# Twelve modulation pieces of a two-block transformer kernel redistributed over VectorE, TensorE and two later places

## The chip, the core and the metric

The kernel runs on one core of one Trainium2 chip. The metric is the device time of one execution in microseconds (us), as the median of several runs. Engines are named as the profile names them: PE is TensorE, PEld its weight loads, DVE is VectorE, ACT is ScalarE, POOL is GpSimd, SP is SyncE, whose queue issues nearly all weight loads. One launch computes the whole model; the weights (380 MB are moved in all, most of it the experts) come from HBM as they are needed.

## What is computed

Two blocks on T = 256 tokens of width D = 1024, everything in float32. Ahead of each block stands a modulation: six vectors ("pieces") of 1024 numbers, each one the product of a 1024-vector with a 1024 x 1024 slice of a weight.

```python
mod = jax.nn.silu(c) @ w_ada[l] + b_ada[l]                   # block one; c_2, w_ada_2, b_ada_2 for block two
sh1, sc1, g1, sh2, sc2, g2 = jnp.split(mod[:, None, :], 6, axis=-1)
h = layer_norm(x) * (1.0 + sc1) + sh1
mix = hybrid_mixer(h, w_in, ...)                             # state-space scan (SSD), short conv, gates, w_o
x = layer_norm(ALPHA * x + g1 * mix) * ln1_g + ln1_b
h = layer_norm(x) * (1.0 + sc2) + sh2
ffn = moe_ffn(h, ...)                                        # router, 8 of 64 experts, a shared expert
x = layer_norm(ALPHA * x + g2 * ffn) * ln2_g + ln2_b
...
h = modulate(rms_norm(x), shift_mix, scale_mix)              # block two
mixed = concat([rms_norm(attn_a) * g_a, rms_norm(attn_b) * g_b]) @ w_out
x = x + gate_mix * mixed
h = modulate(rms_norm(x), shift_ffn, scale_ffn)
gate, val = split(causal_depthwise_conv(h @ w_up, conv_w, conv_b), 2)
x = rms_norm(x + gate_ffn * ((silu(gate) * val) @ w_down)) * final_g
```

A piece is written (b, n) below: b = 0 or 1 for the block, n = 0 to 5 in the order of the split. So (0,2) is g1, (1,0) is shift_mix, (1,2) is gate_mix, (1,3) is shift_ffn, (1,5) is gate_ffn.

## The kernel before

The program is one straight line of stages, each bound to a stretch of the span: modulation (0,0) and (0,1) and the input norm (0 to 37 us); x, the 16 projections that feed the SSD scan (37 to 146); s, 12 projections with the scan's steps woven in (146 to 242); o, the 4 projections `pyb` of the short convolution's output, still with scan steps (242 to 286); z (286 to 342); g, the gates (342 to 396); u, the SSD output projection (396 to 443); `pmix`, the product with w_o, then the first norm and the router (443 to 492); the mixture of experts (492 to 976); the turn to block two, with its norm and the transposes `hb_tp` (976 to 1006); projections and two attentions (1006 to 1140); the up projection with 22 products (1140 to 1269); the down projection and the final norm (1269 to 1339).

A projection is `lin_fm` (L554 to L556): for each of 16 tiles three matmuls, hi x hi, lo x hi and hi x lo. Weights come in float32 and are split on the way: ACT copies the upper part (`whi`, L194) and DVE subtracts it (`wlo`, L198), both per 128 x 1024 half of a 1 MB tile.

Loads go through the class `Stream` (L28). Requests are put in a list in program order; `pump` issues them on SP strictly in that order, each as soon as a buffer of its ring is free: 5 buffers `wraw`, and around the experts 6 `mraw` and 3 `whl`. A request that finds no free buffer holds up all that follow. SP's order is the written one. On the other engines the order of instructions is fixed when the program is built, by a scheduler that may move independent instructions, and each engine executes its queue in order: an instruction that waits holds up all that stand behind it on its engine.

A modulation piece has two forms. Form one is on PE (`ada_piece`, L394, matmuls L403): for each of the four 1 MB tiles of the piece 8 matmuls with the silu(c) column, spread to 32 columns in the constant tile `cst` (L184), as the stationary operand. It is used for (0,0) and (0,1). Form two is on DVE (`ada_tick`, L406): for each of the piece's 8 rows of 128 one SCALAR_TENSOR_TENSOR accumulates weight x silu(c) into `adac` (L430); the first row is done on ACT (L428); at the end PE sums over the partitions with a ones matrix (L435), DVE adds the bias (L390) and ACT's queue writes the 4 KB result to `mod_scr` in HBM (L459). Whoever needs the piece reads it back from there through POOL's queue. In form two a tile is loaded where a string of 0 and 1 says so, one digit for each projection of the stages x, s, o, z, g and u, and consumed at the same place:

```python
XS, SS, OS, ZS, GS, US = [[int(c) for c in a] for a in
                          "0110110110110110,010101010101,1111,11111111,11111111,10101010".split(",")]
```

So 10 pieces, 40 tiles of 1 MB, go through DVE there: 10 tiles in x, 6 in s, 4 in o, 8 in z, 8 in g and 4 in u.

At the turn SP's list holds the last experts' tiles, the two rows of the second norm (`ln2`), the relative-position bias (two gathers from `rel_scr`, L1259 and L1260, into an `mraw` buffer) and the tiles of w_in_2 (L213). PE turns the bias into `bt` (L1659); ACT splits the first w_in_2 tile (L194), takes the squares of the norm (L1683) and scales (L1687); POOL raises to the power -0.5 (L1685); PE transposes `hb_tp` (L1695); ACT and DVE make `hb_f`, `hbh` and `hbl` from it (L493, L494, L486); then the first product `pqb` of block two starts.

Of the kernel before, what the change touches and what calls it, by code (L numbers as in the profile page):

```python
# [25 lines left out]
D = 1024  # L26
# [8 lines left out]
class Stream:  # L35
# [86 lines left out]
def build(ctx, tc, I, out, dbg=None, stop=None):  # L122
# [61 lines left out]
    cst = glob.tile([128, 8, 32], F32, name="cst")  # L184
    V.tensor_copy(cst, csil[:, :8, None].to_broadcast([128, 8, 32]))
# [59 lines left out]
    def req_ada_tile(b, piece, k0):  # L245
        w = I["w_ada_2" if b else "w_ada"][0]

        def f(t):
            n = 2 if (b, piece, k0) == (0, 1, 6) else 1
# [7 lines left out]
        ada_q[b, piece, k0] = ws.add(f, None)  # L257

    def req_ada(b, piece):
        for k0 in range(0, 8, 2):  # L260
# [8 lines left out]
                              "0110110110110110,010101010101,1111,11111111,11111111,10101010".split(",")]  # L269
# [122 lines left out]

    def ada_piece(b, pc):
# [3 lines left out]
        for k0 in range(0, 8, 2):  # L397
            i = ada_q[b, pc, k0]
            w = ws.take_raw(i)
            wv = w.rearrange("p (k n) -> p k n", k=2)  # L400
            for k in range(2):
                for j in range(4):
                    PE.matmul(p[32 * j:32 * j + 32, :256], cst[:, 8 * b + k0 + k, :], wv[:, k, 256 * j:256 * j + 256],  # L403
                              start=(k0 + k == 0), stop=(k0 + k == 7), tile_position=(0, 32 * j))
            ws.done(i)
# [357 lines left out]
    for i in range(4):  # L763
# [365 lines left out]
    rstd(a0, 1e-5)  # L1129
    b0 = first_shift(0, a0)  # L1130
# [4 lines left out]
    G.dma_start(g2, bsrc(scr[5]))  # L1135
    first_scale(1, a1)
# [14 lines left out]
    pr0 = logits(0)  # L1151

# [10 lines left out]
    neg_exp(0, pr0)  # L1163
    scores(0)
# [348 lines left out]
    def prepare_loads():  # L1513

        for k, pc in enumerate((0, 1, 3, 4)):
# [211 lines left out]
    def proj_fm(nm, scale):  # L1727
# [165 lines left out]
    G.dma_start(gfx[:, 0, :], bsrc(scr[11]))  # L1893
# [19 lines left out]
    for i in range(11):  # L1913
# [17 lines left out]
        defer(evac_v)  # L1931
    flush()
# [53 lines left out]
```

## Time and profile before

| what | value |
|---|---|
| median of 3 runs | 1338.19 us (1337.98 to 1346.47) |
| the profiled execution's own time | 1340.41 us |
| its span, first to last instruction | 1338.5 us |
| outside the span | 1.91 us |
| PE busy | 1268.3 us, 95% of the span |
| DVE busy | 813.3 us, 61% |
| ACT, POOL busy | 562.1 us, 178.9 us |
| mean granted clock of PE | 0.979 of full speed |
| moved by DMA | 380.18 MB, 284 GB/s over the span |

The table is an average over stages with different limits. [...]

### The profile page before, as it was taken

Reading aid. Unit: us, or ns where it says so; the run is one execution under the profiler, and the core shown is the slowest. Engines: PE = TensorE matmul, PEld = TensorE weight load, DVE = VectorE, ACT = ScalarE, POOL = GpSimd, SP = SyncE. Lnnn points to the kernel's source line nnn. Section 1 sums busy time; section 2 is a strip of 40 time slices with the busy share of each in tenths; the row PEclk is TensorE's granted clock in tenths of the full one; section 3 lists DMA queues with packets and bytes.
Section 4 is the critical chain, followed back from the end, with each engine's and each line's share of the span. In section 5 each row is a group of like instructions: output and inputs, shape, how many; then the busy total and the mean of one; then the engine's idle time right before and its main releaser. Section 6 shows DMA issues by size and latency. Waiting matters only on the chain.

```text
span 1338.5 us, 22545 instructions
## 1 busy us (share of the span) xinstructions
PE 1268.3 (95%) x8998; PEld 1029.2 (77%) x8998; DVE 813.3 (61%) x1306; ACT 562.1 (42%) x849; POOL 178.9 (13%) x169
## 2 busy tenths in 40 slices
PE   4999999999999989999999999999979999999997
PEld 1898988788899777657576767476549876999986
DVE  2899998977898862222322222222264677788995
ACT  0666644445654342313131313132245655666643
POOL 1002233421100000211112111112120000000000
PEclk9899999999999979999999999999998999899999
DMA  9977766759889288999999999999995334455450
GB/s 337 306 248 252 255 218 225 244 192 311 259 283 345 89 331 314 399 417 418 418 418 416 402 415 419 377 420 403 417 344 177 126 126 138 146 189 185 164 187 32
DMA packets 148975, 380.18 MB, mean 284 GB/s; under 512 B 7839, under 2 KB 97285, under 8 KB 129028
## 3 DMA queue, kind: packets, MB, share of 16 engines
q1 hardware_dynamic: 145856, 373.20, 75.3%
q0 software_dynamic: 2240, 5.34, 1.2%
q8 instruction: 71, 1.16, 0.4%
q10 hardware_dynamic: 772, 0.19, 0.1%
q14 instruction: 36, 0.29, 0.1%
HBM read 377.59 MB, written 1.10 MB: 283 GB/s over the span
## 4 chain that ended last, share of the span: by engine, by line
PE 62%; DVE 5%; DMA 4%; issue 1%; ACT 1%; POOL 0%; SPq 0%; DVEq 0%; POOLq 0%; ACTq 0%
PE gu L1442 16%; PE dn L1473 8%; PE xgp L1400 5%; PE sc L1495 4%; PE pgt L554 2%; PE pgt L555 2%; PE pgt L556 2%; PE pvl L554 2%; PE pvl L556 2%; PE pvl L555 2%; PE pf L906 1%; PE pf L908 1%; PE pf L904 1%; DVE wlo L198 1%; DMA wraw<-in_w_down_dram 1%
## 5 line engine op out<-in xcount | busy, mean ns | idle before, releaser
L194 ACT ACTIVATE whi<-wraw 128x1024 fp32r<-128x1024 f32 x216 | 228.1, 1058 | 244.2 <-PE pf L908 30.8
L198 DVE TENSOR_TENSOR wlo<-wraw,whi 128x1024 fp32r<-128x1024 f32 x216 | 271.3, 1258 | 68.0 <-ACT whi L194 66.6
L1442 PE MATMUL gu<-mraw,xg 128*32 128x256 f32 (+2 forms) x976 | 135.1, 381 | 0.0
L1483 POOL TENSOR_TENSOR y<-yf,y 128x512 fp32r<-128x512 f32 x60 | 76.8, 1280 | 420.9 <-ACT y L1482 420.8
L1452 DVE SCALAR_TENSOR_TENSOR act<-act,gc,gu 128x256 f32<-128x256 f32 x31 | 14.9, 480 | 192.9 <-ACT act L1451 192.9
L1482 ACT ACTIVATE y<-yf 128x512 fp32r<-128x512 f32 x62 | 39.0, 630 | 160.3 <-DVE yf L1481 160.3
L1442 PEld LDWEIGHTS gu<-mraw,xg 128*32 128x32 f32 (+2 forms) x976 | 86.7, 135 | 22.7 <-issue 5.3
L1442 PE MATMUL gu<-wraw,xg 128*32 128x256 f32 (+2 forms) x704 | 98.7, 381 | 0.0
L1481 DVE TENSOR_TENSOR yf<-dn,g 128x512 f32<-128x512 f32 x62 | 42.9, 692 | 66.1 <-PE dn L1473 66.1
L556 PE MATMUL pl<-hh,wlo 128*128 128x256 f32 x256 | 74.4, 292 | 4.2 <-DVE wlo L198 4.1
L1442 PEld LDWEIGHTS gu<-wraw,xg 128*32 128x32 f32 (+2 forms) x704 | 58.2, 129 | 24.1 <-issue 3.9
L555 PE MATMUL pl<-hl,whi 128*128 128x256 f32 x256 | 73.8, 288 | 0.0
L554 PE MATMUL pl<-hh,whi 128*128 128x256 f32 x256 | 73.7, 288 | 0.0
L430 DVE SCALAR_TENSOR_TENSOR adac<-wraw,csil,adac 128x1024 f32<-128x1024 f32 x49 | 66.6, 1359 | 5.1 <-DMA wraw<-in_w_ada_dram 4.6
L1495 PE MATMUL sc<-y,S 128*128 128x512 f32 x248 | 63.3, 404 | 1.4 <-ACT y L1482 0.8
L1495 PEld LDWEIGHTS sc<-y,S 128*128 128x128 f32 x248 | 45.5, 188 | 17.6 <-issue 4.4
L1451 ACT ACTIVATE act<-gu 128x256 f32<-128x256 f32 x31 | 11.9, 383 | 107.3 <-PE gu L1442 107.3
L1402 ACT ACTIVATE xg<-xgp,mvp 128x512 f32<-128x512 f32 (+1 forms) x64 | 48.8, 764 | 18.7 <-PE xgp L1400 18.5
L1400 PE MATMUL xgp<-D,x2h 128*128 128x512 f32 (+1 forms) x128 | 55.0, 429 | 1.4 <-DVE D L1119 1.4
L1473 PE MATMUL dn<-mraw,aT 128*32 128x512 f32 (+2 forms) x200 | 55.2, 596 | 0.0
L556 PEld LDWEIGHTS pl<-hh,wlo 128*128 128x128 f32 x256 | 49.6, 194 | 6.2 <-DVE wlo L198 5.8
L1400 PE MATMUL xgp<-D,x2l 128*128 128x512 f32 (+1 forms) x128 | 53.0, 414 | 0.4 <-DVE x2l L1069 0.4
(575 smaller groups left out, 3531.7 us busy)
## 6 DMA issues: line engine op xcount, KB each, us to landing
wraw<-in_w_in_dram SPq DMA_DIRECT2D x56, 1024.0 KB, 6.4
wraw<-in_w_ada_dram SPq DMA_DIRECT2D x47, 1024.0 KB, 7.2
wraw<-in_w_up_dram SPq DMA_DIRECT2D x44, 1024.0 KB, 5.3
wraw<-in_w_down_dram SPq DMA_DIRECT2D x37, 1024.0 KB, 9.9
mraw<-in_w_up_dram SPq DMA_DIRECT2D x32, 1024.0 KB, 14.5
mraw<-in_w_gate_dram SPq DMA_DIRECT2D x28, 1024.0 KB, 7.1
mraw<-in_w_down_dram SPq DMA_DIRECT2D x23, 1024.0 KB, 17.3
wraw<-in_w_gate_dram SPq DMA_DIRECT2D x21, 1024.0 KB, 15.2
```

The lines of the kernel that those rows point to most:

```text
L194: A.activation(hi, v, AF.Copy)
L198: V.tensor_sub(lo, v, hi.bitcast(F32))
L430: V.scalar_tensor_tensor(acc, wv[:, k, s_], c, acc, op0=OP.mult, op1=OP.add)
L554: PE.matmul(o, wh[:, k, :], xh[:, k0 + k, :], start=(k == 0), stop=False)
L555: PE.matmul(o, wh[:, k, :], xl[:, k0 + k, :], start=False, stop=False)
L556: PE.matmul(o, wl[:, k, :], xh[:, k0 + k, :], start=False, stop=(k == 7))
L1400: PE.matmul(p[:, :c1 - c0], src[:, t, j::8], Dt[:, t, c0:c1], start=(q == 0), stop=(q == 3))
L1402: A.activation(xg[:, j, c0:c1], p[:, :c1 - c0], AF.Identity, scale=mvp[:, 1, j:j + 1], bias=mvp[:, 0, j:j + 1])
L1442: PE.matmul(p[c * k:c * k + c, off:off + 256], xg[:, j, 128 * bb + c * k:128 * bb + c * k + c], wt[j], start=(j == 0), stop=(j == 7), tile ...
L1473: last_dn[0] = PE.matmul(pd[h][c * k:c * k + c, :], aT[:, j, c * k:c * k + c], wt[j][:, 512 * h:512 * h + 512], start=(j == 0), stop=(j == ...
L1483: last_sub[0] = (V if b >= LAST else G).tensor_sub(y[:, 1, hs_], yf[:, h, :], y[:, 0, hs_].bitcast(F32))
L1495: PE.matmul(p, St[:, bb + m, 128 * t:128 * t + 128], y[:, k, 512 * h:512 * h + 512], start=(q == 0), stop=(q == 2 * len(ys) - 1))
```

## The change

The same 12 pieces are computed, in other places:

- VectorE keeps 20 of its 40 tiles: the pieces (0,3), (0,4), (0,5), (1,1) and (1,4), beside z (8 tiles), g (8) and u (4, now at the odd places instead of the even ones). The stages x, s and o have none any more. The first two of these pieces are accumulated in whole rows (`ADA_WIDE = 2`), the others in halves.
- (0,2) is done on PE in o: 8 matmuls after each of the four `pyb` projections.
- (1,0) is done on PE between w_o and the experts: two tiles after the first norm statistics (`rstd(a0)`), two after the first half's router product (`logits(0)`). Its bias goes by POOL, the sum and the write to `mod_scr` by DVE and ACT; ACT's copy `x2h` of half 0 moves ahead of `scores(0)`.
- (1,3) is done on PE at the turn, ahead of the `bt` matmuls. Its four tiles are requested behind the bias and ahead of w_in_2, three into `whl` buffers and one into `wraw`. Then come the bias add on DVE, a write to `mod_scr` from ACT's queue and a read back into `mv2` through POOL's queue.
- (1,2) and (1,5) go through DVE in block two (`late_tick`): a tile after each of the products qb (second), kb (two) and vb, and after the up projection's steps 1, 3, 5 and 7.
- The constant tile `cst` goes; the silu(c) column is read 32 times by a broadcast instead.

The diff, cut to its core:

```diff
@@ Stream.pump
+            if type(tag) is tuple:
+                tag = next((g for g in tag if g in self.free), tag[0])
@@
-                              "0110110110110110,010101010101,1111,11111111,11111111,10101010".split(",")]
+                              "0000000000000000,000000000000,0000,11111111,11111111,01010101".split(",")]
-    ada_tiles = [... [(0, n) for n in range(2, 6)] + [(1, n) for n in range(6)] ...]
+    ada_tiles = [... [(0, 3), (0, 4), (0, 5), (1, 1), (1, 4)] ...]
+    late_ada = [(pc, k0) for pc in (2, 5) for k0 in range(0, 8, 2)]
-    ADA_WIDE = 7
+    ADA_WIDE = 2
@@ requests
         req_cols(I["w_sc_out"][0], 256 * i)
-        req_ada_at("o", i)
+        req_ada_tile(0, 2, 2 * i)
...
         req_rows(I["w_o"][0], 2 * i, gated("g1"))
+    for k0 in range(0, 8, 2):
+        req_ada_tile(1, 0, k0)
@@
+    def ada_rows(p, b, pc, k0):
+        i = ada_q[b, pc, k0]
+        w = raw_rows(i, 2)
+        for k in range(2):
+            for j in range(4):
+                PE.matmul(p[32 * j:32 * j + 32, :256], csil[:, 8 * b + k0 + k:8 * b + k0 + k + 1].to_broadcast([128, 32]), w[k][:, 256 * j:256 * j + 256],
+                          start=(k0 + k == 0), stop=(k0 + k == 7), tile_position=(0, 32 * j))
+        ws.done(i)
@@ stage o
         lin_fm(p, vh, vl)
-        ada_tick("o", i)
+        ada_rows(po, 0, 2, 2 * i)
         step(4)
+    ada_row(ada_end(0, 2, po), 0, 2)
@@ first norm and router
     rstd(a0, 1e-5)
+    pa10 = pacc("ada1_0")
+    ada_rows(pa10, 1, 0, 0)
+    ada_rows(pa10, 1, 0, 2)
...
     pr0 = logits(0)
+    ada_rows(pa10, 1, 0, 4)
+    ada_rows(pa10, 1, 0, 6)
...
     neg_exp(0, pr0)
+    A.activation(x2h[:, 0, :], xnm[:, 0, :], AF.Copy)
     scores(0)
...
+    V.tensor_add(ra[:, 1, :], pa10[:, :256], ra[:, 0, :])
     neg_exp(1, pr1)
+    ada_row(ra[:, 1, :], 1, 0)
@@ requests of the turn and of block two
     bias_req = ws.add(load_bias, None, "mraw")
+    for k0 in range(0, 8, 2):
+        req_ada_tile(1, 3, k0, ("whl", "wraw"))
...
+            req_late((blk, i) != (3, 0))
...
+        req_late(i in (1, 3, 5, 7))
@@ the turn
+    p13 = paux("ada1_3")
+    for k0 in range(0, 8, 2):
+        ada_rows(p13, 1, 3, k0)
+    with tc.issue_after(var[1].ins):
+        V.tensor_add(r13, p13[:, :256], bl_)
+    ada_row(r13, 1, 3)
     for c in range(4):
         p = (plin if c else pacc)(f"bt{c}")
...
+    G.dma_start(mv2[:, 2, :], scr[9].rearrange("(p j) -> p j", j=8))
@@ block two
+    def late_tick(n=1):
+            ...
+                if k0 + k == 0:
+                    A.activation(late_acc, wv[:, k, :], AF.Copy, scale=c)
+                else:
+                    V.scalar_tensor_tensor(late_acc, wv[:, k, :], c, late_acc, op0=OP.mult, op1=OP.add)
```

What this moves on the engines is shown at three places. The first is VectorE's queue in stage s, up to the first scan step's `Cs`, for which PE waits. `wlo` is the lower half of a weight, `adac` an accumulation of form two, `E0_1` and `Cs0` the factors of the scan's first step. Before:

```order
L198 TENSOR_TENSOR wlo36_1666<-wraw37_1466,whi36_1665 128x1024
L430 SCALAR_TENSOR_TENSOR adac_308<-wraw36_1400,csil_99,adac_308 128x1024
L689 TENSOR_TENSOR E0_1_1702<-E0_1_1702,CBm0_1609 128x512
L430 SCALAR_TENSOR_TENSOR adac_308<-wraw36_1400,csil_99,adac_308 128x1024
L198 TENSOR_TENSOR wlo37_1720<-wraw37_1466,whi37_1719 128x1024
L198 TENSOR_TENSOR wlo38_1752<-wraw38_1473,whi38_1751 128x1024
L704 TENSOR_TENSOR Cs0_1715<-Cs0_1715,BC_306 128x512
```

and with the change:

```order
L198 TENSOR_TENSOR wlo36_1605<-wraw26_1274,whi36_1604 128x1024
L709 TENSOR_TENSOR E0_0_1570<-E0_0_1570,CBm0_1548 128x512
L198 TENSOR_TENSOR wlo37_1655<-wraw26_1274,whi37_1654 128x1024
L198 TENSOR_TENSOR wlo38_1687<-wraw27_1343,whi38_1686 128x1024
L709 TENSOR_TENSOR E0_1_1637<-E0_1_1637,CBm0_1548 128x512
L724 TENSOR_TENSOR Cs0_1650<-Cs0_1650,BC_304 128x512
```

The accumulations no longer stand among the scan's factors; the splits (`wlo`) still do.

The second place is SP's queue at the turn, from the second gather of the bias on. Before:

```order
L1260 DMA mraw304_9215<-rel_scr 64x8x256
L213 DMA wraw305_9218<-in_w_in_2_dram 128x8x256
L213 DMA wraw306_9220<-in_w_in_2_dram 128x8x256
L213 DMA wraw307_9222<-in_w_in_2_dram 128x8x256
L213 DMA wraw308_9224<-in_w_in_2_dram 128x8x256
L221 DMA wraw309_9226<-in_w_in_2_dram 128x4x512
```

and with the change:

```order
L1286 DMA mraw292_9180<-rel_scr 64x8x256
L251 DMA whi_293_9183<-in_w_ada_2_dram 128x1024
L251 DMA wlo_293_9184<-in_w_ada_2_dram 128x1024
L251 DMA whi_294_9187<-in_w_ada_2_dram 128x1024
L251 DMA wlo_294_9188<-in_w_ada_2_dram 128x1024
L251 DMA whi_295_9191<-in_w_ada_2_dram 128x1024
L251 DMA wlo_295_9192<-in_w_ada_2_dram 128x1024
L255 DMA wraw296_9195<-in_w_ada_2_dram 128x2x1024
L213 DMA wraw297_9197<-in_w_in_2_dram 128x8x256
L213 DMA wraw298_9199<-in_w_in_2_dram 128x8x256
L255 DMA wraw299_9201<-in_w_ada_2_dram 128x2x1024
L213 DMA wraw300_9203<-in_w_in_2_dram 128x8x256
```

Four 1 MB tiles of (1,3), three of them as pairs of halves, now stand ahead of the first tile of w_in_2, and the first tile of (1,2) ahead of the third.

The third place is the norm of the turn on POOL and on VectorE; `hb_ss` is the norm's sum of squares, `mv2` the modulation columns, `hb_f` the modulated input, `late_acc` the accumulation of (1,2). POOL before:

```order
L991 TENSOR_TENSOR mva_4330<-mva_4330,cneg_87 128x1
L1652 MEMSET mraw304_9215 64x8x64
L991 TENSOR_TENSOR mva_4330<-mva_4330,cneg_87 128x1
L1685 TENSOR_TENSOR hb_ss0_9518<-hb_ss0_9518,cneg_87 128x1
L1685 TENSOR_TENSOR hb_ss1_9523<-hb_ss1_9523,cneg_87 128x1
L1715 DMA gmx_9578<-mod_scr 128x1024
```

and with the change:

```order
L1006 TENSOR_TENSOR mva_4248<-mva_4248,cneg_87 128x1
L1689 MEMSET mraw292_9180 64x8x64
L1693 MEMSET bias13_9463 128x256
L1694 DMA bias13_9463<-in_b_ada_2_dram 4x256
L1006 TENSOR_TENSOR mva_4248<-mva_4248,cneg_87 128x1
L1713 DMA mv2_5270<-mod_scr 128x8
L1738 TENSOR_TENSOR hb_ss0_9540<-hb_ss0_9540,cneg_87 128x1
L1738 TENSOR_TENSOR hb_ss1_9545<-hb_ss1_9545,cneg_87 128x1
```

VectorE with the change (before, the same rows follow each other without the three of `late_acc`):

```order
L198 TENSOR_TENSOR wlo121_9620<-wraw297_9197,whi121_9619 128x1024
L1787 SCALAR_TENSOR_TENSOR late_acc_9601<-wraw299_9201,csil_99,late_acc_9601 128x1024
L513 TENSOR_SCALAR hb_f0_9555<-hb_tp0_9550,mv2_5270 128x256
L513 TENSOR_SCALAR hb_f1_9565<-hb_tp1_9560,mv2_5270 128x256
L1787 SCALAR_TENSOR_TENSOR late_acc_9601<-wraw301_9501,csil_99,late_acc_9601 128x1024
L506 TENSOR_TENSOR hbl_9537<-hb_f0_9555,hbh_9536 128x512
L506 TENSOR_TENSOR hbl_9537<-hb_f1_9565,hbh_9536 128x512
L1787 SCALAR_TENSOR_TENSOR late_acc_9601<-wraw301_9501,csil_99,late_acc_9601 128x1024
L513 TENSOR_SCALAR hb_f2_9575<-hb_tp2_9570,mv2_5270 128x256
L513 TENSOR_SCALAR hb_f3_9585<-hb_tp3_9580,mv2_5270 128x256
L506 TENSOR_TENSOR hbl_9537<-hb_f2_9575,hbh_9536 128x512
```

The read of `mv2` from `mod_scr` now stands ahead of both powers on POOL; on ACT the write to `mod_scr` that it reads stands between the two splits of w_in_2's first tile and the first square of the norm, and one row of (1,2) ahead of the first `hb_f`. On VectorE three accumulations stand among the `hb_f` and `hbl`.

## Rows read from the trace of the kernel before

**Rows 1.** Windows by stage: length, busy us of PE, PEld, DVE, ACT, POOL, PEclk, DMA share, GB/s.

```profile
37.00:146.00 109.00, 104.79 (x827) 101.37 (x826) 101.69 (x171) 70.87 (x98) 10.95 (x8) 0.96 0.81 266
146.00:242.00 96.00, 91.33 (x757) 85.90 (x756) 90.52 (x107) 46.76 (x68) 33.87 (x22) 0.98 0.70 229
242.00:286.00 44.00, 39.42 (x324) 34.39 (x323) 39.25 (x41) 18.12 (x29) 17.45 (x15) 1.00 0.67 219
...
396.00:443.00 47.00, 46.70 (x389) 45.77 (x389) 42.01 (x53) 21.09 (x25) 1.83 (x3) 1.00 0.87 310
...
492.00:976.00 484.00, 482.33 (x3275) 321.79 (x3277) 129.25 (x284) 119.05 (x220) 79.14 (x68) 1.00 0.99 402
976.00:1006.00 30.00, 19.44 (x111) 13.05 (x107) 21.57 (x47) 15.82 (x25) 8.22 (x8) 0.93 1.07 334
1006.00:1140.00 134.00, 129.21 (x810) 108.90 (x810) 86.88 (x137) 77.02 (x127) 4.55 (x6) 0.96 0.41 141
1140.00:1269.00 129.00, 129.00 (x1057) 128.77 (x1057) 108.02 (x157) 79.44 (x111) 0.00 (x0) 0.98 0.52 172
```

**Rows 2.** What PE waited for, 37 to 286 us: us in total, times, longest.

```profile
PE yp L715 <- DVE Cs L704: 6.2, 4, 2.1
PE pl L556 <- DVE wlo L198: 4.1, 5, 2.9
```

**Rows 3.** Timeline of DVE in stage s, up to the first Cs: start, us, what.

```profile
180.83 2.06 DVE L430 SCALAR_TENSOR_TENSOR adac<-wraw,csil,adac 128x1024 f32<-128x1024 f32 x1
182.81 2.06 DVE L198 TENSOR_TENSOR wlo<-wraw,whi 128x1024 fp32r<-128x1024 f32 x1
184.79 0.68 DVE L704 TENSOR_TENSOR Cs<-Cs,BC 128x512 f32<-128x512 f32 x1
```

**Rows 4.** Groups of DVE, 37 to 286 us: busy us, mean ns, idle before.

```profile
L430 DVE SCALAR_TENSOR_TENSOR adac<-wraw,csil,adac 128x1024 f32<-128x1024 f32 x40 | 55.0, 1375 | 2.0 <-DMA wraw<-in_w_ada_dram 1.9
```

**Rows 5.** Windows in which PE's clock falls: columns as in rows 1.

```profile
100.00:110.00 10.00, 7.09 (x46) 6.88 (x46) 9.23 (x9) 6.39 (x8) 6.56 (x4) 0.83 0.71 225
182.00:192.00 10.00, 7.90 (x61) 7.39 (x60) 8.50 (x12) 2.24 (x4) 1.78 (x1) 0.83 0.67 213
475.00:485.00 10.00, 8.70 (x32) 7.95 (x33) 6.60 (x30) 5.27 (x10) 0.69 (x2) 0.55 1.01 419
```

**Rows 6.** Timeline of PE at the start: two tiles of (0,1) in form one.

```profile
24.36 1.97 PE L403 MATMUL ada<-wraw,cst 128*32 128x256 f32 x32
```

**Rows 7.** Groups of PE, the whole span: the ones matmuls of seven pieces.

```profile
L435 PE MATMUL ada<-adac,ones_r 128*32 128x256 f32 x56 | 5.2, 390 | 0.0
```

**Rows 8.** Timeline of DVE in stage u, its longest wait.

```profile
416.67 1.41 DVE L430 SCALAR_TENSOR_TENSOR adae<-wraw,csil,adae 128x512 f32<-128x512 f32 x2 [3.41 <-DMA wraw<-in_w_ada_dram]
```

**Rows 9.** Timeline of PE in norm and router: the two holes that the change fills.

```profile
469.66 1.16 PE L1045 MATMUL h2tp<-ident,xb 128*128 128x128 f32 x8 [2.15 <-DVE xb L1039]
476.30 1.97 PE L1045 MATMUL h2tp<-ident,xb 128*128 128x128 f32 x8 [1.94 <-DVE xb L1039]
```

**Rows 10.** Timeline of SP's queue at the turn: issue, us that the issues stretch over.

```profile
978.18 15.58 SPq L213 DMA_DIRECT2D wraw<-in_w_in_dram  x4
```

**Rows 11.** DMA from 960 to 1040 us, in slices of 2 us: GB/s.

```profile
GB/s 406 434 401 424 424 414 426 410 430 418 408 328 170 209 206 307 351 347 348 349 361 386 387 351 92 0 0 108 379 45 128 376 21 164 357 3 209 315 10 271
```

**Rows 12.** Timeline of ACT, POOL and PE at the turn.

```profile
994.01 2.00 ACT L194 ACTIVATE whi<-wraw 128x1024 fp32r<-128x1024 f32 x2 [0.24 <-DMA wraw<-in_w_in_dram]
997.97 0.55 POOL L1685 TENSOR_TENSOR hb_ss<-hb_ss,cneg 128x1 f32<-128x1 f32 x1 [2.33 <-DVE hb_ss L1684]
1000.11 0.95 POOL L1715 DMA_DIRECT2D gmx<-mod_scr  x1
1005.95 0.58 PE L554 MATMUL pqb<-hbh,whi 128*128 128x256 f32 x1 [3.79 <-DVE hb_f L493]
```

**Rows 13.** DMA issues of 4 KB, the whole span: KB each, median us to landing.

```profile
bada<-in_b_ada_dram POOLq DMA_DIRECT2D x12, 4.0 KB, 5.1
mvp<-mod_scr POOLq DMA_DIRECT2D x2, 4.0 KB, 3.0
```

More of the change, by code (lines that the diff above doesn't have):

```diff
@@ L243, in bsrc, with req_ada_tile @@
         return bass.AP(tensor=ap.tensor, offset=ap.offset, ap=[[0, 128], [1, n]])
-    def req_ada_tile(b, piece, k0):
+    def req_ada_tile(b, piece, k0, tag="wraw"):
         w = I["w_ada_2" if b else "w_ada"][0]
         def f(t):
+            if type(t) is list:
+                for m in range(2):
+                    nc.sync.dma_start(t[m], w[(k0 + m) * 128:(k0 + m + 1) * 128, piece * 1024:(piece + 1) * 1024])
+                return
             n = 2 if (b, piece, k0) == (0, 1, 6) else 1
@@ L391, in ada_end, with raw_rows @@
         return r
+    def raw_rows(i, nj):
+        t = ws.take_raw(i)
+        if type(t) is not list:
+            v = t.rearrange("p (j n) -> p j n", j=nj)
+            return [v[:, j, :] for j in range(nj)]
+        v = [h.rearrange("p (j n) -> p j n", j=nj // 2) for h in t]
+        return [v[2 * j // nj][:, j % (nj // 2), :] for j in range(nj)]
+    def ada_rows(p, b, pc, k0):
[6 more added lines that the diff above has]
+        ws.done(i)
     def ada_piece(b, pc):
@@ L397, in ada_piece @@
         for k0 in range(0, 8, 2):
[L398 to L405, printed above, removed]
+            ada_rows(p, b, pc, k0)
         return ada_end(b, pc, p)
@@ L1135, in build @@
     G.dma_start(g2, bsrc(scr[5]))
+    ra = moe.tile([128, 4, 256], F32, tag="D", name="ra", bufs=1)
+    G.memset(ra[:, 0, :], 0.0)
+    a = I["b_ada_2"][0]
+    G.dma_start(ra[0:128:32, 0, :], bass.AP(tensor=a.tensor, offset=a.offset, ap=[[256, 4], [1, 256]]))
     first_scale(1, a1)
@@ L1267, in build, with req_late @@
     bias_req = ws.add(load_bias, None, "mraw")
+    for k0 in range(0, 8, 2):
+        req_ada_tile(1, 3, k0, ("whl", "wraw"))
     w_in2 = I["w_in_2"][0]
+    def req_late(n=1):
+        for _ in range(n):
+            req_ada_tile(1, *late_ada[late_next[0]])
+            late_next[0] += 1
     for blk in (3, 4):
@@ L1513, in prepare_loads @@
     def prepare_loads():
[L1515 removed]
+        for k, pc in ((0, 0), (1, 1), (3, 4)):
             with tc.issue_after(last_sub[0].ins):
@@ L1652, in build @@
         G.memset(biasT[0:64, :, 0:64], -1e30)
-    pbt = []
+    bl_ = moe.tile([128, 256], F32, tag="act", name="bias13", bufs=2)
+    a = I["b_ada_2"][0]
+    with tc.issue_after(power[0].ins):
+        G.memset(bl_, 0.0)
+    G.dma_start(bl_[0:128:32, :], bass.AP(tensor=a.tensor, offset=a.offset + 3072, ap=[[256, 4], [1, 256]]))
+    pbt = []
+    gap_order = tc.manual_schedule(engines={mybir.EngineType.SP, mybir.EngineType.PE})
+    gap_order.__enter__()
+    p13 = paux("ada1_3")
+    for k0 in range(0, 8, 2):
+        ada_rows(p13, 1, 3, k0)
+    r13 = moe.tile([128, 256], F32, tag="act", name="r13", bufs=2)
+    with tc.issue_after(var[1].ins):
+        V.tensor_add(r13, p13[:, :256], bl_)
+    ada_row(r13, 1, 3)
     for c in range(4):
@@ L1713, in build @@
     rows["gmx"] = sec.tile([128, D], F32, name="gmx")
+    late_acc = sec.tile([128, D], F32, name="late_acc")
+    late_b = sec.tile([128, 256], F32, name="late_b")
     with tc.issue_after(last[3].ins):
-        G.dma_start(rows["gmx"], bsrc(scr[8]))
+        G.memset(late_b, 0.0)
+    def late_tick(n=1):
+        for _ in range(n):
+            pc, k0 = late_ada[late_next[1]]
+            late_next[1] += 1
+            if k0 == 0:
+                a = I["b_ada_2"][0]
+                G.dma_start(late_b[0:128:32, :], bass.AP(tensor=a.tensor, offset=a.offset + pc * 1024, ap=[[256, 4], [1, 256]]))
+            i = ada_q[1, pc, k0]
+            wv = ws.take_raw(i).rearrange("p (k n) -> p k n", k=2)
+            for k in range(2):
+                c = csil[:, 8 + k0 + k:9 + k0 + k]
+                if k0 + k == 0:
+                    A.activation(late_acc, wv[:, k, :], AF.Copy, scale=c)
+                else:
+                    V.scalar_tensor_tensor(late_acc, wv[:, k, :], c, late_acc, op0=OP.mult, op1=OP.add)
+            ws.done(i)
+            if k0 < 6:
+                continue
+            p = plin(f"ada1_{pc}")
+            for j in range(4):
+                PE.matmul(p[32 * j:32 * j + 32, :256], ones_r.bitcast(F32)[:, :32], late_acc[:, 256 * j:256 * j + 256],
+                          start=True, stop=True, tile_position=(0, 32 * j))
+            r = wk.tile([128, 256], F32, tag="adar", name=f"adar1_{pc}")
+            V.tensor_add(r, p[:, :256], late_b)
+            A.dma_start(scr[6 + pc].rearrange("(j n) -> j n", j=4), r[0:128:32, :])
+            G.dma_start(rows["gmx" if pc == 2 else "gfx"], bsrc(scr[6 + pc]))
     tri_lt = sec.tile([128, 2, 128], F32, name="tri_lt")
```

26 lines of the change are left out of this document (12 added, 14 removed).

## The prediction

> **What bounds the kernel now.** I read the table of windows first, cut at the stages, because the page's average (PE busy 95%) mixes stages with different limits. The reader is to compare each row's length with its PE and DVE columns [rows 1]. In x, s and o PE falls short of the stage by 4.21, 4.67 and 4.58 us, 13.5 us in all, while VectorE is busy 101.69 of 109, 90.52 of 96 and 39.25 of 44 us: 93%, 94% and 89%. In u VectorE is also at 89%, yet PE lacks only 0.3 us of 47: there no scan step waits for it. In the experts PE is full (482.33 of 484) and so is DMA (0.99). At the turn PE works 19.44 of 30 us. In the up projection PE is full.
>
> Second, PE's waits from 37 to 286 us: the two largest name VectorE, 6.2 us for the scan's `Cs` and 4.1 us for `wlo` [rows 2]. Third, VectorE's timeline ahead of the first `Cs`: an accumulation of 2.06 us and a split stand right before it [rows 3], so part of the wait is the queue that the change empties. The accumulations of x, s and o are 40 instructions of 1375 ns, 55.0 us [rows 4], of 231.5 us that VectorE works there: without them its load falls from 93% to 71%. [...]
>
> **Stages x, s and o.** The most that can come back is 13.5 + 3.4 = 16.9 us. Not all of it will: the scan step is a chain over PE, ACT, POOL and VectorE, and the splits of VectorE still stand between its links. From below, a quarter comes back (-4), if the waits are the chain's own latency. Since both large waits end on VectorE and its load falls to less than in u, I take three quarters: -12.7. PE's own work stays about level. The piece (0,2) adds four tiles at 1.97/2 us [rows 6], +3.9; five pieces fewer end here with a ones product of 5.2/7 = 0.74 us each [rows 7], -3.7. The broadcast column in place of the constant tile is in no row; I cost it at nothing, and at +3.9 if it doubled the tiles' time.
>
> **Stage u.** The ticks move from even to odd places, so the last sits one projection nearer to the product with w_o. In their favour, VectorE waited 3.41 us for a tile at an early one [rows 8]; against them, this work now falls nearer the end. PE had 0.3 us of idle here, so nothing can be won; the loss is at most two tiles' worth of accumulation, four times 1375 ns less the 3.41, or 2 us. I take +0.5.
>
> **Norm and router.** PE waits 2.15 and 1.94 us for `xb` [rows 9]; two tiles of (1,0) take 1.97 us at full clock and twice that at the lower level. If they fill the holes exactly nothing is lost; at half clock the two sets overrun by 2 x (3.9 - 2.0) = +3.8 us. On the other side the clock there is 0.55 over 475 to 485 us [rows 5], after PE had stood still twice: at full clock those 10 us hold 5.5 us of pulses, a gain of up to 4.5. I take -1, near nothing, as both signs are of one size.
>
> [...]
>
> **The experts** keep their instructions and are full on PE and DMA [rows 1]: 0, within 1.5.
>
> **The turn** is where the change pays. SP issues the bias, then w_in_2, and the issues stretch over 15.58 us [rows 10]; ACT waits for the first tile until 994.01 [rows 12]. Behind it, in order on ACT, stand the splits, the squares and the scaling, on which POOL, the transposes and the first `pqb` (1005.95) hang. Now four tiles, 4.19 MB, stand ahead of w_in_2 in the same queue. The queue moves 418 GB/s in the 22 us before the bias and 347 to 387 behind it [rows 11], so the first w_in_2 tile comes 4.19/0.418 = +10.0 us later (9.7 at 434 GB/s, 12.1 at 347). The 32 small matmuls of (1,3) follow each tile as it lands, 1 us each [rows 6], and end before w_in_2 is there; `bt` then runs while ACT splits. So neither is on the path.
>
> POOL comes next. The read of `mv2` stands ahead of both powers and waits for ACT's write to land, which is issued only after the two splits. Before, the first power starts 1.96 us after the splits end (996.01 to 997.97) [rows 12]. Now it starts after a 4 KB transfer's way to landing, 3.0 to 5.1 us [rows 13], and the read's own issue, about 0.95 us [rows 12]: 3.0 + 0.95 - 1.96 = +2.0 to +4.1. I take +2.5, nearer to the row that reads the same scratch.
>
> VectorE has three accumulations of 1375 ns [rows 4] among `hb_f` and `hbl`; one may lie in VectorE's wait for the transposes, so 2.75 to 4.1, and I take +3.5. Sum of the turn: 10.0 + 2.5 + 3.5 = +16.0. From above 12.1 + 4.1 + 4.1 = 20.3; from below 9.7, if POOL and VectorE find cover. `pqb` would start about 1022 - 13 (all that comes before) on the new span.
>
> **Block two.** (1,2) lies beside attention and projections, where VectorE is busy 86.88 of 134 us [rows 1]: nothing. (1,5) adds 7 accumulations of 1375 ns, 9.6 us, to 108.02 of 129 us [rows 1], VectorE at 91%. PE has no idle there now. At 93% in x PE lost 4.1 us to late splits [rows 2], but there the scan's work came in lumps. I take +1, from 0 to +5.
>
> **Sum.** -12.7 + 0.2 + 0.5 - 1 + 0 + 16.0 + 1 = +4.0 us on the profiled execution's 1340.41 us, of which 1338.5 is the span and 1.91 lies outside: 1344.4. The median of the runs is 2.2 us lower, 1338.19; on that scale 1342.
>
> **Rivals.**
> A. The gain is whole and the turn is cheap. PE fills all of x, s and o (-16.9), the router's clock rises (-4), and at the turn only the transfer counts (+9.7), with u and block two at 0: -11.2, 1327. For it: in u PE is full at VectorE's 89%. Against it: a quarter of what remains on VectorE still stands in one queue with the scan, and POOL's wait has nothing to hide under.
>
> B. The turn decides: ACT's small write takes its place behind SP's backlog. When it is issued, three tiles (w_in_2, the first of (1,2), w_in_2 again) are on their way, 3.15 MB or 9.0 us at 350 GB/s. If the write had to wait for them, POOL's power would come 9.0 us later than above: turn +25, total +13, 1351, slower. It decides from about 4 us of extra landing on: the turn is then +20, the total +8, and the first block pays for less than two thirds of the turn. For it: the bias on SP's own queue and the stream share the same engines. Against it: 4 KB on POOL's queue landed in 5.1 us in the median, with DMA busy 0.67 to 0.81 in x to o [rows 1, 13].
>
> [...]
>
> C. The change moves the work, but PE's waits were the scan's own latency: only a quarter of the 16.9 comes back, -4.2 in place of -12.7, and the total is +12.5, 1350.5. For it: the waits for `Cs` recur with each step. Against it: rows 3, where an accumulation stands right ahead.
>
> **How the numbers follow.** The forecast with its neighbourhood (1335 to 1348) has 0.57, A 0.16, B 0.10, C 0.17. The range leaves out the outer half of A and of B's and C's upper ends, where the turn reaches 20.3 as well: 1327 to 1355. A change of 1%, 13.4 us, is about what a measurement of this kernel can tell from none. Faster by more than that needs A with more than its own sum: 0.08. Slower by more needs B or C with the turn's upper bound or a block two at +5: 0.15. Within 1%: 0.77.
>
> **What would show it.** In the changed profile: x to o shorter by about 12 us, with the waits for `Cs` and `wlo` under half; PE's clock at 1.00 where it was 0.83; no `adac` before z. Router: the two waits for `xb` under 1 us. Turn: the first split of w_in_2 about 10 us later relative to the last expert product, the first power 3 to 5 us after the splits, three `late_acc` among `hb_f`, `pqb` 16 us later on that scale. Up projection: PE waits for `wlo` of no more than a few us. Wrong it would be if w_in_2 lands as early as before, if the waits of the scan stay, or if POOL's read is long done when the power starts.

## The result, and the profile after

The changed kernel takes 1357.14 us (median of 4 runs, 1355.95 to 1358.67); the kernel before, on the same chip, 1339.91 us (1337.98 to 1346.47, now 4 runs). The ratio of the means is 1.012, with a 95% interval of 1.0097 to 1.0142: slower by 1.2%. The forecast was 1342, its range ended at 1355. The profiled execution took 1355.95 us, its span is 1354.1 us, 15.6 over the 1338.5 of before.

The table of windows comes first again, now cut at each stage's first product in the changed kernel (columns as in [rows 1]): x, s, o, g, u, from the last expert product to the first product of block two, and the up projection.

```profile
36.50:132.90 96.40, 96.40 (x794) 95.73 (x794) 85.52 (x154) 63.66 (x90) 5.05 (x4) 0.99 0.65 203
132.90:225.60 92.70, 90.64 (x757) 86.40 (x756) 74.60 (x90) 45.22 (x66) 31.78 (x23) 1.00 0.44 137
225.60:270.90 45.30, 43.13 (x379) 35.84 (x377) 30.73 (x34) 18.37 (x30) 15.60 (x13) 1.00 0.59 197
...
326.90:387.60 60.70, 56.64 (x420) 52.44 (x419) 50.10 (x73) 32.20 (x41) 3.90 (x6) 0.94 0.76 246
387.60:439.00 51.40, 48.53 (x393) 47.81 (x392) 43.14 (x54) 21.82 (x27) 1.82 (x3) 0.97 0.85 305
...
978.70:1017.10 38.40, 22.48 (x154) 11.55 (x153) 18.55 (x41) 13.26 (x19) 6.10 (x10) 0.78 0.95 310
...
1155.00:1284.20 129.20, 129.06 (x1064) 128.29 (x1065) 114.58 (x164) 80.69 (x112) 0.57 (x1) 0.99 0.63 208
```

x is now full on PE (96.40 of 96.40), at clock 0.99. But g, in which VectorE accumulates 8 tiles as before, has 4 us of PE idle and a clock of 0.94, and u has 2.9 us of idle. Stage g in the kernel before:

```profile
341.80:395.80 54.00, 52.79 (x420) 49.26 (x419) 48.90 (x71) 31.85 (x41) 3.71 (x6) 1.00 0.81 264
```

g has become 6.7 us longer: PE stands still for 2.9 us more and takes 3.9 us more for the same products, at a granted clock of 0.94 where it was 1.00. The same cut in all the traces, from one stage's first product to the next (us; "product, router" begins with the product with w_o, "turn" runs from the last expert product to the second product of block two, "rest" to the end of the span):

| stage | before | changed | e1 | e2 | e3 | e4 | e5 | e6 | e7 | e8 | e9 |
|---|---|---|---|---|---|---|---|---|---|---|---|
| start to z | 285.9 | 270.9 | 271.7 | 271.8 | 273.7 | 270.7 | 271.3 | 277.4 | 275.9 | 270.9 | 271.6 |
| z | 56.0 | 56.1 | 55.7 | 55.7 | 55.7 | 55.7 | 55.7 | 55.7 | 55.7 | 55.7 | 55.7 |
| g | 53.9 | 60.6 | 53.2 | 62.1 | 58.7 | 58.3 | 62.2 | 53.8 | 53.8 | 53.2 | 53.2 |
| u | 47.7 | 51.4 | 50.1 | 48.4 | 49.4 | 52.9 | 50.9 | 47.7 | 50.4 | 48.1 | 48.2 |
| product, router | 48.3 | 48.6 | 48.3 | 48.6 | 49.5 | 47.3 | 49.5 | 49.9 | 47.2 | 49.9 | 49.9 |
| experts | 490.0 | 491.1 | 491.1 | 491.2 | 490.8 | 491.7 | 491.7 | 491.2 | 492.9 | 490.9 | 491.8 |
| turn | 32.5 | 49.1 | 49.0 | 50.8 | 34.2 | 46.2 | 47.7 | 32.8 | 32.9 | 49.1 | 40.4 |
| rest | 324.1 | 326.3 | 328.0 | 329.4 | 326.9 | 330.8 | 326.7 | 326.1 | 325.4 | 327.9 | 330.7 |
| span | 1338.5 | 1354.1 | 1347.0 | 1357.9 | 1339.0 | 1353.5 | 1355.8 | 1334.5 | 1334.3 | 1345.7 | 1341.5 |

Up to z the change wins 15.0 us. It gives back 6.7 in g, 3.7 in u, 0.3 up to the experts, 1.1 in them, 16.6 at the turn and 2.2 behind it: 15.6 in all.

What PE waits for, from 36 to 271 us (first fence; the split's 4.1 us of [rows 2] are gone, and of `Cs` 2.5 us are left of 6.2) and from 271 to 440 (second):

```profile
PE yp L735 <- DVE Cs L724: 2.5, 3, 1.0
```

```profile
PE pya L576 <- DVE wlo L198: 2.9, 1, 2.9
PE pg L576 <- DVE wlo L198: 2.7, 2, 1.9
```

Loads that came late are no rival for the gain ahead of z: from 37 to 286 us the kernel before waited for a load only twice, 3.0 us on ACT and 1.9 us on VectorE, each time for a tile of an accumulation.

In g, PE waits for a split on VectorE. VectorE's and POOL's timelines there show why the split is late. Before:

```profile
345.14 1.16 POOL L857 DMA_DIRECT2D mvp<-mod_scr  x2
351.58 0.15 DVE L858 TENSOR_SCALAR mvp<-mvp 128x8 f32<-128x8 f32 x1
```

and with the change:

```profile
331.15 0.59 POOL L881 DMA_DIRECT2D mvp<-mod_scr  x1
334.44 0.54 POOL L881 DMA_DIRECT2D mvp<-mod_scr  x1 [2.14 <-DMA mod_scr<-adar]
340.24 0.17 DVE L882 TENSOR_SCALAR mvp<-mvp 128x8 f32<-128x8 f32 x1 [6.30 <-DMA mvp<-mod_scr]
340.32 1.23 DVE L198 TENSOR_TENSOR wlo<-wraw,whi 128x1024 fp32r<-128x1024 f32 x1
```

`mvp` holds the pieces (0,3) and (0,4) as columns for the router. In the kernel before they ended on VectorE in x and s, were written to HBM at 123.71 and 174.76 us, and VectorE did not wait for the read. Now (0,4) ends with z, its write is under way when POOL wants to read (2.14 us of wait), and VectorE stands 6.30 us at an instruction of 0.17 us, the +1 on these columns (the factor 1 + sc2), which stands ahead of the split PE needs. The router that uses it comes 120 us later.

In u it is an accumulation that waits for its tile, ahead of the split for which PE waits 2.9 us (VectorE):

```profile
404.56 0.69 DVE L506 TENSOR_TENSOR ml<-mg,mh 128x512 fp32r<-128x512 f32 x1
412.04 0.75 DVE L450 SCALAR_TENSOR_TENSOR adae<-wraw,csil,adae 128x512 f32<-128x512 f32 x1 [6.79 <-DMA wraw<-in_w_ada_dram]
412.71 1.22 DVE L198 TENSOR_TENSOR wlo<-wraw,whi 128x1024 fp32r<-128x1024 f32 x1
```

The wait of 3.41 us at the even place [rows 8] was hidden; 6.79 us at the odd one is not. In the router both holes of [rows 9] are filled (0.29 us is left of 2.15, nothing of 1.94), the second set of matmuls takes 3.50 us, with the granted clock at 0.50 from 469 to 472 us, where the first takes 1.93 at 1.00, and a new hole of 1.70 us opens ahead of the shared expert (PE):

```profile
461.75 1.93 PE L416 MATMUL ada<-wraw,csil 128*32 128x256 f32 x32
463.97 1.16 PE L1060 MATMUL h2tp<-ident,xb 128*128 128x128 f32 x8 [0.29 <-DVE xb L1054]
...
468.61 3.50 PE L416 MATMUL ada<-wraw,csil 128*32 128x256 f32 x32
...
478.02 6.25 PE L1092 MATMUL sh<-h2f,mraw 128*128 128x256 f32 x20 [1.70 <-issue]
```

At the turn the last expert product starts at 978.72 (981.86 before). The lines of PE, ACT, POOL and VectorE that answer to [rows 12]:

```profile
998.25 1.93 PE L416 MATMUL ada<-wraw,csil 128*32 128x256 f32 x16 [1.54 <-DMA wraw<-in_w_ada_dram]
1001.38 2.00 ACT L194 ACTIVATE whi<-wraw 128x1024 fp32r<-128x1024 f32 x2 [10.24 <-issue]
1005.94 0.99 ACTq L479 DMA_DIRECT2D mod_scr<-r  x1
1006.97 1.06 ACT L1736 ACTIVATE hb_x<-x 128x1024 f32<-128x1024 f32 x1 [3.59 <-issue]
1009.68 0.60 POOL L1713 DMA_DIRECT2D mv<-mod_scr  x1 [15.62 <-DMA mod_scr<-r]
1010.31 1.13 POOL L1738 TENSOR_TENSOR hb_ss<-hb_ss,cneg 128x1 f32<-128x1 f32 x2
1014.60 1.28 DVE L1787 SCALAR_TENSOR_TENSOR late_acc<-wraw,csil,late_acc 128x1024 f32<-128x1024 f32 x1 [1.22 <-ACT late_acc L1785]
1017.06 0.39 PE L574 MATMUL pqb<-hbh,whi 128*128 128x256 f32 x1 [1.60 <-ACT hbh L506]
```

The splits of w_in_2 start 22.66 us after the last expert product, where it was 12.15 (994.01 - 981.86): the transfer costs 10.5. From their end the first power starts after 6.93 us instead of 1.96: +5.0. The write is issued only 2.56 us after the splits; its landing takes 3.19 us by the chain of work that ended last:

```profile
1005.94 3.19 DMA mod_scr<-r
```

The first product of block two starts 38.3 us after the last expert product, 14.3 more than before. Before, it started when all of its input was there; now it starts on the first half and waits inside for the rest, so the table measures the turn up to the second product.

### The profile page after: what moved, and what is told of

It reads as the page before. It is cut to its first block, busy times and chain, and to the rows that moved or that the text cites. A ratio compares the mean times of both kernels' runs of the same rounds, so it can differ in the third digit from the quotient of the medians.

```text
span 1354.1 us, 22889 instructions
## 1 busy us (share of the span) xinstructions
PE 1281.4 (95%) x9166; PEld 1032.1 (76%) x9166; DVE 792.9 (59%) x1284; ACT 557.5 (41%) x844; POOL 172.1 (13%) x172
## 5 line engine op out<-in xcount | busy, mean ns | idle before, releaser
L1479 PE MATMUL gu<-wraw,xg 128*32 128x256 f32 (+2 forms) x736 | 135.0, 381 | 0.0
L1479 PEld LDWEIGHTS gu<-wraw,xg 128*32 128x32 f32 (+2 forms) x736 | 82.1, 135 | 31.0 <-issue 5.3
L1510 PE MATMUL dn<-wraw,aT 128*32 128x512 f32 (+2 forms) x192 | 59.1, 596 | 1.3 <-DMA wraw<-in_w_down_dram 1.3
L1437 PE MATMUL xgp<-D,x2l 128*128 128x512 f32 (+1 forms) x128 | 53.2, 415 | 0.4 <-DVE x2l L1084 0.4
L574 PE MATMUL pgt<-h3h,whi 128*128 128x256 f32 x176 | 50.6, 288 | 1.5 <-ACT h3h L506 1.5
## 6 DMA issues: line engine op xcount, KB each, us to landing
mraw<-in_w_down_dram SPq DMA_DIRECT2D x23, 1024.0 KB, 15.6
```

The costliest lines, as they stand in the source:

```text
L574: PE.matmul(o, wh[:, k, :], xh[:, k0 + k, :], start=(k == 0), stop=False)
L1437: PE.matmul(p[:, :c1 - c0], src[:, t, j::8], Dt[:, t, c0:c1], start=(q == 0), stop=(q == 3))
L1479: PE.matmul(p[c * k:c * k + c, off:off + 256], xg[:, j, 128 * bb + c * k:128 * bb + c * k + c], wt[j], start=(j == 0), stop=(j == 7), tile ...
L1510: last_dn[0] = PE.matmul(pd[h][c * k:c * k + c, :], aT[:, j, c * k:c * k + c], wt[j][:, 512 * h:512 * h + 512], start=(j == 0), stop=(j == ...
```

## The experiments

Theory: most of the forecast's terms held, and what it lacked is one wait in g (VectorE at a read-back) and the size of the wait in u. Rival for g and u: weight tiles landed late there whatever VectorE does. For the turn, the rival is that accumulations and the clock made it long, not the loads.

**e1_mvp.** The +1 leaves stage g:

```diff
-    V.tensor_scalar(mvp[:, 1, :], mvp[:, 1, :], 1.0, None, op0=OP.add)
@@ stage u
-            V.tensor_add(m, m, yb[:, sl, :])
+            ws.merged = V.tensor_add(m, m, yb[:, sl, :])
@@ behind stage u
+    with tc.issue_after(ws.merged.ins):
+        V.tensor_scalar(mvp[:, 1, :], mvp[:, 1, :], 1.0, None, op0=OP.add)
```

> The changed kernel with one VectorE instruction moved: the +1 on the router's modulation columns (mvp) stands behind stage u's last merge instead of in stage g. Theory (VectorE's queue stood still 6.3 us behind the read-back of pieces that now end later): the two slow gate projections (12.8 and 9.0 us) return to 8.2 and 6.9 us, and the whole kernel is 5 to 7 us faster than the changed one (1354.1 us span, so 1347 to 1349). Rival (the gates are late because their weight tiles land late): both projections stay within 1 us of what they were and the span within 1 us.

Measured: ratio to the kernel before 1.0101 (1.007 to 1.0132), span of the profiled execution 1347.0. Stage g by the table of windows:

```profile
327.30:380.60 53.30, 53.18 (x420) 49.38 (x419) 49.88 (x71) 32.11 (x41) 3.89 (x6) 1.00 0.84 280
```

PE is full, at clock 1.00, with the same VectorE work (49.88 against 50.10 us). The theory holds for the stage, with 7.4 us in g; the other kernels that keep the instruction in g take 58.3 to 62.2 us there, those without it 53.2 to 53.8. The span of the two traces differs by 7.1 us, but the five runs scatter from 1347.95 to 1357.34, and their ratio is not clear of the change's. In the times of the runs the gain shows only in e8.

**e2_ueven.** `US` is 10101010 again.

> The changed kernel with the four ticks of stage u back at the even places. Theory (the odd place puts an accumulation that waits 6.8 us for its tile ahead of the split that PE needs next): the fifth u projection falls from 10.4 to about 6 us, the span by 3 to 4 us. Rival (the tile is late because of three other 512 KB reads in the same stretch, wherever the tick stands, and PE pays for it): the u stage stays within 1 us and so does the span.

Measured: ratio 1.0105 (1.0077 to 1.0134), span 1357.9. In u the theory holds: 51.4 falls to 48.4. Over all traces u takes 49.4 to 52.9 us with the ticks at the odd places and 47.7 to 48.4 with them at the even ones. VectorE's wait is shorter here and two ticks lie behind it:

```profile
410.99 1.41 DVE L450 SCALAR_TENSOR_TENSOR adae<-wraw,csil,adae 128x512 f32<-128x512 f32 x2 [3.83 <-DMA wraw<-in_w_ada_dram]
```

The span did not follow: the profiled execution is the slowest of the four runs (1351.62 to 1359.67), and it lost 1.5 us in g, where nothing was edited, 1.7 at the turn and 3.1 behind it. So this kernel does not price u for the whole.

**e3_x13.** (1,3) moves from the turn to VectorE beside x: `XS` is 0001001000010010, its requests behind the bias, its matmuls, write and read-back at the turn go, and `mv2` is read with the other columns.

> The changed kernel with piece (1,3) taken from the turn and accumulated on VectorE beside x (four ticks); its loads no longer stand ahead of w_in_2, and there is no write and read-back at the turn. Theory (at the turn the four tiles cost 10.5 us of transfer and the read-back 5 us): from the last expert product to the first product of block two 38 falls to 23 to 25 us, x costs at most 1.5 us more, and the span falls by 13 to 15 us, to 1339 to 1341. Rival (the turn is long for the three accumulations and for the clock, not for the loads): the span falls by less than 8 us.

Measured: ratio 1.0025 (1.0009 to 1.0041), span 1339.0, 15.1 less. The first w_in_2 tile is there for ACT 12.8 us after the last expert product (977.9):

```profile
990.68 2.00 ACT L194 ACTIVATE whi<-wraw 128x1024 fp32r<-128x1024 f32 x2 [0.41 <-DMA wraw<-in_w_in_dram]
```

The turn falls from 49.1 to 34.2, 1.7 over the kernel before. x costs 2.5 us more, one more than expected. The theory holds; the edit takes the loads and the read-back away together and does not part their costs.

**e4_late.** The accumulations of (1,2) are held behind the norm:

```diff
+                    with tc.issue_after(last[2].ins):
                         A.activation(late_acc, wv[:, k, :], AF.Copy, scale=c)
...
+                    with tc.issue_after(last[4].ins):
                         V.scalar_tensor_tensor(late_acc, wv[:, k, :], c, late_acc, op0=OP.mult, op1=OP.add)
```

> The changed kernel with every accumulation of (1,2) held behind the last hbl of the turn's norm; the loads stay. Theory (three accumulations of 1.28 us stand on the path among hb_f and hbl): the first product of block two comes 3 to 4.5 us earlier and the span falls by 3 to 4 us. Rival (they lie in waits of VectorE for the transposes and for ACT): less than 1 us.

Measured: ratio 1.0112 (1.0084 to 1.014), span 1353.5, 0.6 less. The first product of block two does not come earlier (38.6 us after the last expert product for 38.3). Up to the second one the turn is 2.9 us shorter, but what follows is 4.5 longer. PE's waits from 1012 to 1057 us show the splits late there, for a part of it:

```profile
PE pqb L576 <- DVE wlo L198: 1.4, 1, 1.4
PE pkb L576 <- DVE wlo L198: 1.0, 1, 1.0
```

So neither theory nor rival: the accumulations do stand on the path, inside the first product, but moved back they delay the splits of the next products instead. Held back, they were no gain.

**e5_pool.** ACT's write goes behind its last norm instruction, POOL's read-back behind both powers, and `r13`, the sum of (1,3), gets a buffer that outlives the turn:

```diff
-    r13 = moe.tile([128, 256], F32, tag="act", name="r13", bufs=2)
+    r13 = glob.tile([128, 256], F32, name="r13")
...
-    ada_row(r13, 1, 3)
...
-    G.dma_start(mv2[:, 2, :], scr[9].rearrange("(p j) -> p j", j=8))
...
     last = rms_to_feature(x2, 0, hbh, hbl, "hb", hb_pools)
+    with tc.issue_after(last[0].ins):
+        ada_row(r13, 1, 3)
+    with tc.issue_after(last[3].ins):
+        G.dma_start(mv2[:, 2, :], scr[9].rearrange("(p j) -> p j", j=8))
```

> The changed kernel with the write of (1,3) to scratch behind ACT's last norm instruction, and its read-back behind POOL's two powers (by the way the scheduler puts one accumulation row of (1,2) behind the first hb_f). Theory (ACT's write was issued 2.6 us after the splits ended, only when SP had passed a branch that waits for the second w_in_2 tile, and POOL then waited for its landing): the first power starts 4 to 5 us earlier counted from the last expert product, and the first product of block two 3 to 5 us earlier; at the turn 38 falls to 33 to 35 us. Rival (the write's place on ACT does not matter, as the squares wait for something else): the squares start where they did and the turn stays within 1 us.

Measured, in two runs: ratio 1.0116 (1.0095 to 1.0137), span 1355.8. ACT and POOL:

```profile
1007.35 2.00 ACT L194 ACTIVATE whi<-wraw 128x1024 fp32r<-128x1024 f32 x2 [12.70 <-SPq L1609]
1010.66 0.55 POOL L1736 TENSOR_TENSOR hb_ss<-hb_ss,cneg 128x1 f32<-128x1 f32 x1 [13.07 <-DVE hb_ss L1735]
1011.30 0.99 ACTq L479 DMA_DIRECT2D mod_scr<-r  x1
```

From the end of the splits the power now starts after 1.3 us instead of 6.93: that wait is gone. But the expectation counted from the last expert product, and from there the first power comes only 2.3 us earlier, not 4 to 5, the first product 2.5 us (35.8 for 38.3) and the second 1.4, since the splits themselves start 26.0 us after the last expert product, 3.3 later. PE here also waited 0.97 us inside that product for its weights, so the stream ran later. In e9 the splits are only 1.0 us later than in the change, and the gain shows.

**e6_best and e7_best_odd.** e1's edit, e3's, and also (1,2) beside x (`XS` is 0010101010101011, 8 tiles); (0,2), (1,0) and (1,5) stay where the change put them. e6 has u's ticks at the even places, e7 at the odd ones.

> The changed kernel with mvp's +1 late, the ticks of stage u at the even places, and both (1,3) and (1,2) accumulated on VectorE beside x (8 ticks there), so nothing of them is left at the turn or in the projections of block two; (0,2), (1,0) and (1,5) stay where the change put them. Theory (the freed scan is worth 15 us, and what ate it were g 7, u 3, turn and late accumulations 17): span 1327 to 1332 against 1338.5 of the kernel before, 0.4 to 0.8% faster. Rival (8 tiles beside x bring the waits of x back): x at 105 us or more, no faster than before.

> As e6_best, with stage u's ticks left at the odd places. Theory: the u stage is 2 to 3 us longer than in e6_best, the rest the same, span 1329 to 1335. Rival (once g is mended, SP's stream is ahead and the tile at the odd place is there in time): within 1 us of e6_best.

Measured: e6 1335.11 us against 1340.3 for the kernel before in the same runs, ratio 0.9954 (0.994 to 0.9967); e7 0.9953 (0.9939 to 0.9966). Both are faster than both kernels, than the kernel before by half a percent. The spans, 1334.5 and 1334.3, stand at 2.5 us above e6's range and within e7's; x with 8 tiles takes 101.9 us in e6:

```profile
36.70:138.60 101.90, 99.78 (x803) 97.51 (x802) 95.51 (x164) 65.66 (x91) 6.62 (x5) 0.98 0.77 252
```

With VectorE at 94% of the stage, PE is 2.1 us short again. In e7 u is 2.7 us longer than in e6 and the stretch behind it, up to the experts, 2.7 shorter: the place of the ticks makes no difference to the whole here, as the rival had it, though not for its reason.

**e8_mended.** e1's and e2's edits together; the change's turn stays.

> The changed kernel with the two edits of e1_mvp and e2_ueven together; turn and block two as the change has them. Theory (the forecast missed by the wait in g, 6.7 us, and by the size of the term for u, 3.2 instead of 0.5; its other terms hold): span 1343 to 1347, within 2 us of the 1342.4 that the forecast gave as a span and 0.3 to 0.6% over the kernel before. Rival (the two gains do not add, since what g and u give is taken back by the router or the experts): span 1348 or more.

Measured: ratio 1.0065 (1.004 to 1.0091), span 1345.7: g 53.2, u 48.1, turn 49.1 us. The interval lies clear below the change's (1.0097 to 1.0142), so the two waits together are worth it in the times of the runs too. In the stages the gains of 7.4 and 3.3 add; the router takes 1.3 back and what follows the turn 1.6. Against e1, from which only the place of the ticks differs, u is 2.0 shorter and the stretch up to the experts 1.6 longer, as between e7 and e6: how much of u's gain reaches the whole is not shown.

**e9_mended_turn.** e8 with e5's and e4's edits.

> e8_mended with the turn eased as well, (1,3) staying there: the write and the read-back as in e5_pool, the accumulations of (1,2) held behind the norm as in e4_late. Theory (of the turn's 16.5 us only the 10.5 of the transfer cannot be hidden): turn to the second product of block two 43 to 45 us against 49 of the changed kernel and 32.5 of the kernel before, span 1338 to 1342. Rival (the read-back and the accumulations only move to the next stage): span within 1.5 us of e8_mended.

Measured: ratio 1.0026 (1.0011 to 1.0041), span 1341.5. The turn is 40.4 us, better than expected, 7.9 over the kernel before; the rest is 330.7, as in e4, 2.8 more than in e8. What the transfer costs at the turn stays.

## Why the prediction missed

- **Up to z** (-12.5 forecast with PE's own work, -15.0 measured, 0.6 of it ahead of x). The step was right and the share somewhat low: 14.4 us in x, s and o, of the 16.9 that could come back. Rival C is refuted: of the waits for `Cs` and `wlo` 2.5 us are left of 10.3, and the clock is 0.99 and 1.00. No run shows the 3.4 us in the sum's 16.9, an estimate of what the clock costs these stages; what the traces show in its place is the granted clock itself, 0.50 from 104 to 107 and from 186 to 189 us before, and now 0.99 over x and 1.00 over s and o.
- **The step that failed is a term that the sum doesn't have.** The forecast's sum passes from o to u: z and g are put at nothing without a reason. VectorE does accumulate 8 tiles beside each, as before, but the forecast did not ask which pieces end there now and who reads them next. (0,4) now ends with z, and the +1 on its read-back stands on VectorE right behind, ahead of a split that PE needs: +6.7 us, shown by e1 (7.4 back in the stage). The forecast followed the new read-back at the turn and missed that an old one had become late.
- **Stage u** (+0.5 forecast, at most +2; +3.7 measured). The mechanism was named and its size was off: it counted the extra work and took the wait for the tile as a credit of 3.41 us, while the wait grew to 6.79 and now stands ahead of a split. e8 takes 3.3 us back in u; the whole kernel gains less or nothing by it (e8 against e1, e6 against e7).
- **Norm and router** (-1 forecast, +0.3 measured). The holes were filled as described, but the gain from the clock did not come: it is 0.86 from 464 to 487.6 us. The forecast's lower level is a granted clock of 0.50 in the traces, from 476 to 486 us before and from 469 to 472 now; there the second set of (1,0) took 3.50 us, 1.8 times the first one's 1.93 where the forecast had twice. A new hole of 1.70 us opened.
- **The turn** (+16.0 forecast, +16.6 measured). The transfer was 10.5 for 10.0. The read-back was 5.0 for 2.5, beyond its upper bound of 4.1: the landing was inside its rows (3.19), and what the term lacked is the 2.56 us before the issue. The accumulations and what follows come to 1.1 for 3.5. Two errors cancel, so that the sum fits is luck. To the first product, on which the forecast counted, it is +14.3.
- **Rival B** had the landing late behind SP's backlog. It was not: 3.19 us, with two 1 MB tiles on their way, of which the later one, issued 7.6 us ahead of the write, landed 2.0 us after it. B's three tiles ahead of the write did not occur, since the issue itself was late: it waited until one of them had landed (last section). So the backlog did cost something, 2.56 us, by a way that neither the forecast nor B had.
- **Block two and the experts** (+1 and 0 forecast; +2.2 and +1.1 measured): inside their bounds. But the forecast laid its +1 on the up projection, which is as it was, 129.2 us, with VectorE at 89%; 2.1 us lie ahead of it, in the projections and attentions beside (1,2), for which it had nothing. From block two's second product to the up projection it is 125.2 us before and 127.3 now, and 125.9 and 126.3 in e6 and e7, which have (1,2) elsewhere.

On the profiled execution the change came to +15.6 us where the forecast had +4.0. The 11.6 between them are g and z 6.8, u 3.2, router 1.3, block two 1.2, experts 1.1 and the turn 0.6, less 2.5 won before z. The medians lie further apart, 1357.14 against 1342: the forecast took off 2.2 us from the profiled execution to the median, while the changed kernel's profiled execution was its fastest run, 1.2 below its median. Less g's 6.7 us the median would be about 1350, inside the range and still 8 above the forecast. The range held bounds for the waits in the lines that the change adds, and none for readers in lines that it leaves alone.

## What to carry to other kernels

When the producer of a value moves later, list every reader of it, also those in code that the change leaves alone, and look at what is queued behind the first reader on its engine: here 0.17 us of VectorE work, needed 120 us later, cost 7 us in its stage. A wait hidden at one place in a queue says little of the next place: what counts is whether the instruction right behind it is one the bottleneck needs (here VectorE's 3.41 us at the even place left PE 0.3 us of idle in u, its 6.79 at the odd one 2.9). And loads that are put ahead of a stage's first weights cost their full transfer if that stage starts as soon as they land: here 10.5 us for four 1 MB tiles.

## What the hardware showed that I had not expected

- A 4 KB value that goes through HBM took 11.5 us from the issue of its write (ACT's queue, 328.71) to the first use of its read-back (340.24), of which the read took 5.8 us from its issue at 334.44, on queues with the DMA engines 76% busy in the stage.
- ACT's small write at the turn was issued 2.56 us after ACT had finished, in the same moment at which SP went on with its loads (1005.94 and 1006.05). The trace's semaphore events show why. SP's queue passes a branch between the experts and block two (L1609), and there it stood from 1001.26 to 1005.70, on the semaphore of the second w_in_2 tile, which landed at 1005.68. Behind it, at 1005.85, the branch set the semaphore for which ACT's write waited. So this branch, waiting for a load in flight, held up a write on another engine's queue for these 2.56 us; the splits ahead of it started likewise, at 1001.38, when the branch had passed the first w_in_2 tile's semaphore (in e5 the profile names this branch as what released them). No run moves the branch.
- In the router PE's granted clock fell while PE hardly stood still. From 461.75 to 468.61 the longest hole in its timeline is 0.51 us. After the first set of (1,0) it did 8 transposes and 16 small router products; the granted clock is 1.00 from 460 to 465, 0.88 to 470 and 0.78 to 475, with 0.50 from 469 to 472, and the second set took 3.50 us.
